# Hybrid attention encoder on one core: full-attention scores of two heads made together, the products with the low part of K over 64 rows each in two halves of the array

## Chip, cores, metric

The kernel runs on one core of one Trainium2 chip. The metric is device time in microseconds, the median of several runs. In the profile PE is TensorE (PEld its weight loads), DVE is VectorE, ACT ScalarE, POOL GpSimd, SP SyncE, whose queue issues most of the DMA transfers.

## What is computed

One layer of an encoder over 1024 tokens of width 1024. One input projection feeds two groups of heads: group A is full attention (8 query heads of 64 over 2 key heads, normalised and rotated), group B is attention over a neighbourhood on a grid. Both are gated, concatenated, projected and added to the residual. The part that matters here, cut from the reference:

```python
def _gqa_blocked(q, k, v):          # q: 8 heads, k and v: 2 heads, head_dim 64, 1024 tokens
    qb = q.reshape(b, nb, Q_BLOCK, hk, g, d)            # blocks of 128 queries
    def block(qi):
        sc = jnp.einsum('bqkgd,bskd->bkgqs', qi, k).astype(jnp.float32) * scale
        p = jax.nn.softmax(sc, axis=-1).astype(v.dtype)
        return jnp.einsum('bkgqs,bskd->bqkgd', p, v)
```

## The kernel before

Inputs are float32, and TensorE is fed with pairs of float16 numbers: a value is kept as a high part and a low part (what the high part leaves). A projection is three products: high x high, high x low, low x high.

Full attention is a list `ua` of 64 units in the order (hh, u, h): key head hh, block u of 128 queries, one of the four query heads h of that key head. The text calls unit i "head i" and the step in which it is started "step i". For one unit, `a_qk` makes the scores of 128 queries against 1024 keys in a PSUM tile `s` of two banks. The stationary operand `q` has 128 rows: the high part of the query's 64 numbers and the low part, stacked. The moving operand is first `kTa[:, :, hh]`, which holds the high part of K twice, one copy under the other (lines L713, two products of 512 columns: high and low part of q times the high part of K), then K's low part, also held twice (`kTa[:, :, 2]` for hh 0, `klo1` for hh 1; L715, two more products into the same banks). DVE reduces the scores to a row's maximum (L720, with a junk output), ACT makes the exponential in float32 (L722) and its float16 copy (L723), DVE subtracts to get the low part (L728, in `a_lo`, one step later), SP issues one transpose of both parts (L733), and five steps later `a_pv` multiplies with V (L745 to L747, 24 small products). The tiles `s` come from a pool with two buffers.

`Flow` sets the order. Each call of `fl.step` runs, for each engine in program order: pieces due "pre", ACT's jobs, `a_qk` followed by `a_pv` of the unit five back, `a_lo` of the unit before, pieces due "mid", DVE's jobs, and then a number of filler chunks (`fl.fill`). A chunk is six products of 256 columns or three of 512 of a projection that a later stage needs (L482); `FILL_A` and what follows it say how many go into a step (5, then 4.2, then about 3.7). Evacuations of these projections and the splitting of weights into high and low parts (ACT L392, DVE L397) are jobs. In the first six steps the order on ACT, DVE, POOL and SP is left to a list scheduler; from step 6 on it is the order of the program. PE's order is always that of the program.

The first steps overlap with the preparation of the last query tiles: `norm_rope` (DVE L533, L534, POOL L535, DVE L539, POOL L543, DVE L546, POOL L547) and then the staging in `qa_gen`: ACT L562 copies the high part, DVE L563 subtracts the low part, and L566 issues the transpose that puts both into `qTa`. The text calls the stretch from the first scores to 130 us "the head" of the stage.

Group B follows. Its `b_scores` makes scores of two heads together: two products of 128 rows (L804), and then two products of 64 rows with K's low part (L807), one on rows 0 to 63 and one on rows 64 to 127, for which an even head's staged query has its high part in the upper rows and an odd head's in the lower ones.

Of the kernel before, what the change touches and what calls it, by code (L numbers as in the profile page):

```python
# [8 lines left out]
F32 = mybir.dt.float32  # L9
F16 = mybir.dt.float16  # L10
BF16 = mybir.dt.bfloat16
AF = mybir.ActivationFunctionType
OP = mybir.AluOpType
# [3 lines left out]
P = 128  # L17
# [4 lines left out]
D = 64  # L22
# [17 lines left out]
RING, VB1 = 5, 24576  # L40
# [8 lines left out]
class Flow:  # L49
# [12 lines left out]
    def at(self, delay, pos, fn, *a):  # L62
        self.due.setdefault((self.slot + delay, pos), []).append((fn, a))
# [75 lines left out]
def kernel(ctx: ExitStack, tc: tile.TileContext, x: bass.AP, w: bass.AP, wo: bass.AP,  # L139
# [3 lines left out]
    act, dve, pool, pe, sp = nc.scalar, nc.vector, nc.gpsimd, nc.tensor, nc.sync  # L143
# [5 lines left out]
    ps_s = ctx.enter_context(tc.tile_pool(name="ps_s", bufs=2, space=PSUM))  # L149
# [4 lines left out]
    at, job = fl.at, fl.job  # L154
# [8 lines left out]
    ar = one.tile([P, 16928], F32, name="ar")  # L163
# [3 lines left out]
    def carve(store, off, shape, dt):  # L167

        n = 4 if dt == F32 else 2
        t = store[:, off // 4:off // 4 + int(np.prod(shape)) * n // 4]  # L170
        t = t if n == 4 else t.bitcast(dt)
        if len(shape) == 1:
            return t
        names = "abcdef"[:len(shape)]
        return t.rearrange(f"p ({' '.join(names)}) -> p {' '.join(names)}", **dict(zip(names, shape)))
# [6 lines left out]
    def slot(kind, shape, dt):  # L182

        off, size, n = SLOTS[kind]
        k = turn[kind] = turn.get(kind, -1) + 1
        off += k % n * size
        return area(off, shape[1:], dt) if off < AREA else carve(rq, off - AREA, shape[1:], dt)
# [4 lines left out]
    def r6(i, shape, dt, name):  # L192
        if i >= 2:
            return carve(rq, (i - 2) * 6144, shape[1:], dt)
        return one.tile(shape, dt, tag=f"r{i}", name=name)

    def tn(name, n=1, tag="t"):
        return tiny.tile([P, n], F32, tag=tag, name=name)
# [47 lines left out]
    NSA, SHA = 80, 81  # L246

    def col(i, n=1):
        return sm[:, i:i + n]
# [239 lines left out]
    def proj_pair(g, up, lhs, evac):  # L489

        need_w(g)
        pt = proj_tile(f"pj{g}_{up}")
        hi, lo = wp[g]
        trips = ((0, hi), (0, lo), (1, hi))
        if (g, up) in ((KVA, 0), (QA, 0)):
            seq = [(k, a, b) for a, b in ((0, hi), (1, hi), (0, lo)) for k in range(KC)]
        else:
            seq = [(k, a, b) for k in range(KC) for a, b in trips]
        for i in range(2):
            ops = [((pt[:, i], lhs(a, k, 2 * up + i), b[:, k]), dict(start=n == 0, stop=n == 23))  # L500
                   for n, (k, a, b) in enumerate(seq)]
            yield from chunks(ops, 6, (lambda: evac(pt)) if i else None)
# [4 lines left out]
    kTa = r6(0, [P, NU, 3, P], F16, "kTa")  # L507
# [5 lines left out]
    qTa = [carve(rq, 8192 * i, [NU, 4, P], F16) for i in range(2)]  # L513
    klo1 = carve(rq, 16384, [NU, P], F16)
# [39 lines left out]
    def qa_gen(hh, up):  # L554
        def evac(pt):
            g = QA + hh
            stg = slot("stg1", [P, 2, 4, P], F16)
            a, b = (0, D) if hh == 0 else (D, 0)

            def fin(q):  # L560
                d = 3 if hh else 2
                at(d, "pre", lambda: act.activation(stg[:, :, :, a:a + D], q, AF.Copy))  # L562
                at(d, "mid", lambda: dve.tensor_tensor(stg[:, :, :, b:b + D], q, stg[:, :, :, a:a + D], op=OP.subtract))  # L563

                def tr():
                    sp.dma_start_transpose(qTa[hh][:, 2 * up:2 * up + 2].rearrange("p i h t -> p (i h) t"),  # L566
                                           stg.rearrange("p i a b -> p (i a b)"))
                at(d, "post", tr)
            norm_rope(g, up, pt, 4, 0, fin)
        yield from proj_pair(QA + hh, up, from_h, evac)  # L570

    def kva_gen(up):
        def evac(pt):
            both = slot("stg1", [P, 8, P], F16)
            stg, stg_l = both[:, :6].rearrange("p (i a) b -> p i a b", a=3), both[:, 6:]
            vs = pt[:, :, P:].rearrange("p a (h d) -> p a h d", d=D)
            at(1, "pre", lambda: act.activation(va[:, 2 * up:2 * up + 2, :, :D], vs, AF.Copy, scale=2.0 ** -14))

            def vlo():
                for i in range(2):  # L580
                    dve.scalar_tensor_tensor(va[:, 2 * up + i, :, v_lo], vs[:, i], 2.0 ** -14,
                                             va[:, 2 * up + i, :, :D], op0=OP.mult, op1=OP.subtract)
            at(1, "mid", vlo)

            def fin(k):
                def hi():
                    act.activation(stg[:, :, :2, :D], k, AF.Copy)
                    act.activation(stg[:, :, :2, D:], k, AF.Copy)
                at(2, "pre", hi)

                def lo():
                    for h, to in ((0, stg[:, :, 2]), (1, stg_l)):
                        dve.tensor_tensor(to.rearrange("p i (e d) -> p i e d", d=D),
                                          k[:, :, h, None, :].to_broadcast([P, 2, 2, D]),
                                          stg[:, :, h].rearrange("p i (e d) -> p i e d", d=D), op=OP.subtract)
                at(2, "mid", lo)

                def tr():
                    sp.dma_start_transpose(kTa[:, 2 * up:2 * up + 2].rearrange("p i a t -> p (i a) t"),
                                           both[:, :6].rearrange("p a b -> p (a b)"))  # L600
                    sp.dma_start_transpose(klo1[:, 2 * up:2 * up + 2], stg_l.rearrange("p a b -> p (a b)"))
                at(2, "post", tr)
            norm_rope(KVA, up, pt[:, :, :P], 2, 1, fin)
        yield from proj_pair(KVA, up, from_h, evac)
# [94 lines left out]
    def group(g, gens):  # L699

        def first(gen):
            prep(g + 1)
            yield from gen
        return [first(gens[0]) if g < 16 else gens[0], *gens[1:]]


    pv, sums, pts, hls = {}, {}, {}, {}

    def a_qk(i, hh, u, h):
        s = ps_s.tile([P, 1024], F32, tag="s", name=f"s{hh}_{u}_{h}")  # L710
        q = qTa[hh][:, u, h]
        for c in range(2):
            pe.matmul(s[:, c * 512:(c + 1) * 512], q, kTa[:, 4 * c:4 * c + 4, hh], start=True, stop=False)  # L713
        for c in range(2):
            pe.matmul(s[:, c * 512:(c + 1) * 512], q, klo1[:, 4 * c:4 * c + 4] if hh else kTa[:, 4 * c:4 * c + 4, 2],  # L715
                      start=False, stop=True)
        nm = tn(f"nm{hh}_{u}_{h}")
        o = 4096 * (i % RING)
        hl, p32 = carve(ar, o, [2, 1024], F16), carve(ar, o + 2048, [1024], F32)
        dve.tensor_tensor_reduce(out=hl[:, 1].bitcast(BF16), in0=s, in1=col(SHA).to_broadcast([P, 1024]), scale=col(NSA),  # L720
                                 scalar=3e38, op0=OP.add, op1=OP.min, accum_out=nm)
        act.activation(p32, s, AF.Exp, bias=nm, scale=col(SCA))  # L722
        at(0, "mid", lambda: act.activation(hl[:, 0], p32, AF.Copy))  # L723
        hls[hh, u, h] = (hl, p32)

    def a_lo(i, hh, u, h):
        hl, p32 = hls.pop((hh, u, h))
        dve.tensor_tensor(hl[:, 1], p32, hl[:, 0], op=OP.subtract)  # L728
        if i % 4 == 3:
            pt = one.tile([P, 16, P], F16, tag="gain", name=f"pt{hh}_{u}_{h}")  # L730
        else:
            pt = carve(ar, 4096 * RING + 2048 + 4096 * (i % 4), [16, P], F16)
        sp.dma_start_transpose(pt, hl.rearrange("p a b -> p (a b)"))  # L733
        pts[hh, u, h] = pt
# [292 lines left out]
    k, q = [kva_gen(up) for up in UP], group(1, [qa_gen(0, up) for up in UP])  # L1027
# [86 lines left out]
    mid = (CHUNKS_A - sum(n * r for n, r in FILL_A) - FILL_A_END * SKEW_A) / (64 - n_head) + 0.02  # L1114
    fl.base = BASE_A
    with run_units(ua, SKEW_A, a_qk, a_lo, a_pv, rates(FILL_A + [(64 - n_head, mid)], FILL_A_END), by_hand=HAND):
        pass
# [39 lines left out]
    a, b = ORDER[2:4]  # L1157
# [112 lines left out]
```

## Time and profile before

| what | before |
|---|---|
| runs, us | 572.87, 575.61, 575.24; median 575.24 |
| span of the profiled execution, us | 570.8 (its own time isn't listed; the span leaves out what lies before the first and after the last instruction) |
| PE busy | 517.2 us, 91% of the span |
| DVE busy | 459.4 us, 80% |
| ACT busy | 391.7 us, 69% |
| full attention, first to last score product, us | 85.2 to 350.4 |

A busy PE means that some matmul is in flight. Matmuls overlap in the pipeline, so what one costs is read from the distance between starts, not from its duration. Rows of the timeline give start, duration, engine, line, operation, output<-input, shapes, how many instructions are merged, and in brackets how long the engine was idle before and what ended that.

### The profile page before, as it was taken

What the parts mean: (1) busy time and instruction counts of PE and PEld (TensorE: products, weight loads), DVE (VectorE), ACT (ScalarE), POOL (GpSimd) and SP (SyncE); (2) the same over time, 40 slices, a digit from 0 to 9 for tenths busy, and PEclk for the clock granted to TensorE, in tenths of its full rate; (3) what the DMA queues carried; (4) which work ended last, traced back from release to release, by engine and by line L of the source; (5) the groups of instructions that cost most, each with busy time, mean ns of one, the idle gap of its engine ahead of it and who ended that gap; (6) DMA issues with size and microseconds to landing.
All of it is one profiled execution on the core that took longest, in us unless ns stands there. A gap on an engine that the chain in (4) does not pass through costs nothing. (4 is left out here: it accounts for less than half of the span.)

```text
span 570.8 us, 13962 instructions
## 1 busy us (share of the span) xinstructions
PE 517.2 (91%) x5583; PEld 402.1 (70%) x5583; DVE 459.4 (80%) x1018; ACT 391.7 (69%) x615; POOL 150.6 (26%) x181
## 2 busy tenths in 40 slices
PE   2678889969999999999999999999799799997994
PEld 0456777757887555568888888887677577776883
DVE  4688787989887988778779887589978998988852
ACT  5546457667777769687696886387888888875321
POOL 2395786650000000000000022334521311212210
PEclk9979999998999999999999999999989899999998
DMA  8999548779999989998998999436466999899842
GB/s 241 220 175 231 121 91 185 131 144 165 220 180 210 158 204 200 197 196 162 217 191 192 184 160 213 132 52 130 121 121 107 198 216 165 144 176 167 194 109 73
DMA packets 245539, 95.49 MB, mean 167 GB/s; under 512 B 236513, under 2 KB 237025, under 8 KB 243554
## 3 DMA queue, kind: packets, MB, share of 16 engines
q1 hardware_dynamic: 241874, 73.89, 71.1%
q0 software_dynamic: 3312, 19.92, 12.7%
q10 hardware_dynamic: 288, 0.79, 0.5%
q8 instruction: 43, 0.70, 0.5%
q14 instruction: 22, 0.18, 0.1%
HBM read 29.56 MB, written 4.19 MB: 59 GB/s over the span
## 5 line engine op out<-in xcount | busy, mean ns | idle before, releaser
L482 PE MATMUL pj<-whl,hT 128*128 128x256 f16 x2112 | 254.9, 278 | 26.1 <-DMA hT<-ar 9.2
L482 PEld LDWEIGHTS <-hT 128*128 128x128 f16 x2112 | 203.7, 99 | 63.6 <-issue 20.3
L722 ACT ACTIVATE ar<-s,nm,sm 128x1024 f32<-128x1024 f32 x64 | 76.9, 1201 | 56.5 <-DVE nm L720 56.2
L720 DVE CUSTOM_DVE_ANT_0 ar<-s,sm 128x1024 bf16<-128x1024 f32 x64 | 82.0, 1281 | 35.0 <-PE s L715 34.6
L482 PEld LDWEIGHTS <-ar 128*128 128x128 f16 x768 | 73.0, 99 | 16.1 <-issue 7.0
L728 DVE TENSOR_TENSOR ar<-ar 128x1024 f16<-128x1024 f32 x64 | 80.3, 1255 | 0.9 <-ACT ar L723 0.8
L482 PE MATMUL po<-whl,ar 128*128 128x256 f16 x576 | 68.7, 273 | 2.0 <-DVE x2b L961 1.8
L723 ACT ACTIVATE ar<-ar 128x1024 f16<-128x1024 f32 x64 | 67.6, 1057 | 1.9
L828 ACT ACTIVATE rq<-ar,mx,sm 128x384 f32<-128x384 f32 (+1 forms) x64 | 43.0, 672 | 25.3 <-DVE mx L827 25.0
L829 ACT ACTIVATE ar<-ar,mx,sm 128x384 f16<-128x384 f32 (+1 forms) x64 | 43.5, 680 | 2.1
L482 PE MATMUL kb<-hT,whl 128*128 128x512 f16 x192 | 44.5, 379 | 0.0
L834 DVE TENSOR_TENSOR ar<-rq,ar 128x384 f16<-128x384 f32 (+1 forms) x64 | 35.5, 555 | 8.2 <-ACT ar L829 8.0
L746 PE MATMUL pv<-va,ar 128*128 128x64 f16 x384 | 40.6, 195 | 0.0
L745 PE MATMUL pv<-va,ar 128*128 128x65 f16 x384 | 40.5, 194 | 0.0
L747 PE MATMUL pv<-va,ar 128*128 128x65 f16 x384 | 40.4, 193 | 0.0
L713 PE MATMUL s<-kTa,rq 128*128 128x512 f16 x128 | 38.5, 383 | 1.5 <-ACT ar L722 1.4
L745 PEld LDWEIGHTS <-ar 128*128 128x128 f16 x384 | 35.9, 97 | 5.5 <-issue 0.3
L397 DVE SCALAR_TENSOR_TENSOR whl<-raw,sm,whl 128x512 f16<-128x512 f32 x52 | 39.5, 790 | 0.0
L746 PEld LDWEIGHTS <-ar 128*128 128x128 f16 x384 | 35.7, 98 | 5.5 <-issue 0.3
L207 POOL DMA_DIRECT2D raw<-in_w_dram x11 | 6.7, 607 | 113.0 <-ACT ar L723 88.8
L747 PEld LDWEIGHTS <-ar 128*128 128x128 f16 x384 | 35.7, 99 | 0.0
L392 ACT ACTIVATE whl<-raw,sm 128x512 f16<-128x512 f32 x52 | 33.9, 708 | 0.0
(163 smaller groups left out, 918.8 us busy)
## 6 DMA issues: line engine op xcount, KB each, us to landing
raw<-in_w_dram POOLq DMA_DIRECT2D x11, 1024.0 KB, 7.4
raw<-in_wo_dram POOLq DMA_DIRECT2D x4, 1024.0 KB, 5.7
ar<-in_x_dram SPq DMA_DIRECT2D x7, 512.0 KB, 6.3
khh<-ar SPq DMA_DIRECT2D x16, 128.0 KB, 3.5
x2b<-in_x_dram POOLq DMA_DIRECT2D x4, 512.0 KB, 6.1
x<-in_x_dram POOLq DMA_DIRECT2D x4, 512.0 KB, 5.8
out_dram<-x2b SPq DMA_DIRECT2D x8, 256.0 KB, 4.8
ar<-ar SPq DMA_TRANSPOSE x112, 4.3
```

What stands on the lines that cost most here:

```text
L397: dve.scalar_tensor_tensor(wp[g][1][:, q], raw[g][:, q], col(S_ + g), wp[g][0][:, q], op0=OP.mult, op1=OP.subtract)
L482: pe.matmul(*o[0], **o[1])
L713: pe.matmul(s[:, c * 512:(c + 1) * 512], q, kTa[:, 4 * c:4 * c + 4, hh], start=True, stop=False)
L720: dve.tensor_tensor_reduce(out=hl[:, 1].bitcast(BF16), in0=s, in1=col(SHA).to_broadcast([P, 1024]), scale=col(NSA), scalar=3e38, op0=OP.ad ...
L722: act.activation(p32, s, AF.Exp, bias=nm, scale=col(SCA))
L723: at(0, "mid", lambda: act.activation(hl[:, 0], p32, AF.Copy))
L728: dve.tensor_tensor(hl[:, 1], p32, hl[:, 0], op=OP.subtract)
L745: pe.matmul(o, pt[:, kt], va[:, kt, hh, v_hi], start=kt == 0, stop=False)
L746: pe.matmul(o[:, :D], pt[:, kt], va[:, kt, hh, v_lo], start=False, stop=False)
L747: pe.matmul(o, pt[:, 8 + kt], va[:, kt, hh, v_hi], start=False, stop=kt == 7)
L828: act.activation(p32, t, AF.Exp, bias=mx, scale=col(SCB + hh))
L829: act.activation(hl[:, 0], t, AF.Exp, bias=mx, scale=col(SCB + hh))
```

## The change

Scores are made for two units at once, at every even step, by a new function `a_scores`: four products with the high part of K (two per head), then the four with the low part, each over 64 rows: the even head's on rows 0 to 63, the odd head's on rows 64 to 127, alternating. Only the high part of q meets the low part of K now. DVE's reductions of both heads follow one another in that step; the exponential of the second head stays in its own step. For this the staged query of odd heads has its two parts swapped in `qa_gen`, which splits one ACT copy and one DVE subtraction into two each.

```diff
@@ qa_gen
-            a, b = (0, D) if hh == 0 else (D, 0)
+            s6 = stg.rearrange("p i (k e) (b d) -> p i k e b d", e=2, d=D)
...
-                at(d, "pre", lambda: act.activation(stg[:, :, :, a:a + D], q, AF.Copy))
-                at(d, "mid", lambda: dve.tensor_tensor(stg[:, :, :, b:b + D], q, stg[:, :, :, a:a + D], op=OP.subtract))
+                q5 = q.rearrange("p i (k e) d -> p i k e d", e=2)
+                for e in range(2):
+                    at(d, "pre", lambda e=e: act.activation(s6[:, :, :, e, e], q5[:, :, :, e], AF.Copy))
+                    at(d, "mid", lambda e=e: dve.tensor_tensor(s6[:, :, :, e, 1 - e], q5[:, :, :, e], s6[:, :, :, e, e], op=OP.subtract))
...
+    def a_scores(i, hh, u, hs):
+        k_lo = klo1 if hh else kTa[:, :, 2]
+        s = [ps_s.tile([P, 1024], F32, tag="s", name=f"s{hh}_{u}_{h}") for h in hs]
+        q = [qTa[hh][:, u, h] for h in hs]
+        for e in range(2):
+            for c in range(2):
+                pe.matmul(s[e][:, c * 512:(c + 1) * 512], q[e], kTa[:, 4 * c:4 * c + 4, hh], start=True, stop=False)
+        for c in range(2):
+            for e in range(2):
+                r = slice(e * D, e * D + D)
+                pe.matmul(s[e][:, c * 512:(c + 1) * 512], q[e][r], k_lo[r, 4 * c:4 * c + 4], start=False, stop=True)
+        for e, h in enumerate(hs):
+            nm = tn(f"nm{hh}_{u}_{h}")
+            o = 4096 * ((i + e) % RING)
+            hl, p32 = carve(ar, o, [2, 1024], F16), carve(ar, o + 2048, [1024], F32)
+            dve.tensor_tensor_reduce(out=hl[:, 1].bitcast(BF16), in0=s[e], in1=col(SHA).to_broadcast([P, 1024]), scale=col(NSA),
+                                     scalar=3e38, op0=OP.add, op1=OP.min, accum_out=nm)
+            hls[hh, u, h] = (hl, p32, s[e], nm)
+
     def a_qk(i, hh, u, h):
...
+        if h % 2 == 0:
+            a_scores(i, hh, u, (h, h + 1))
+        hl, p32, s, nm = hls[hh, u, h]
         act.activation(p32, s, AF.Exp, bias=nm, scale=col(SCA))
         at(0, "mid", lambda: act.activation(hl[:, 0], p32, AF.Copy))
-        hls[hh, u, h] = (hl, p32)
```

What moves, engine by engine. PE at head 26 (tile `s_6_2`; `s_6_3` is head 27, `pv_5` a probability product, `kb_1_0` a filler). Before, one head's four score products stand between a filler and a probability product:

```order
L482 MATMUL kb_1_0_2504<-hT_99,whl_1740 128x512
L713 LDWEIGHTS rq
L713 MATMUL s_6_2_2515<-kTa,rq 128x512
...
L713 MATMUL s_6_2_2515<-kTa,rq 128x512
L715 LDWEIGHTS rq
L715 MATMUL s_6_2_2515<-kTa,rq 128x512
...
L745 MATMUL pv_5_2457<-va,ar 128x65
```

After, at the same place, both heads' products (L717 with K's high part, L721 with the low part):

```order
L717 MATMUL s_6_2_2531<-kTa,rq 128x512
...
L717 MATMUL s_6_3_2532<-kTa,rq 128x512
...
L721 MATMUL s_6_2_2531<-kTa,rq 128x512
L721 LDWEIGHTS rq
L721 MATMUL s_6_3_2532<-kTa,rq 128x512
...
L756 MATMUL pv_5_2473<-va,ar 128x65
```

Head 27's four products moved up by one step, past the probability products and fillers of step 26, and step 27 has no scores.

DVE at the same place (ISA is the reduction, `nm` its result; L728, after the change L739, the subtraction of the head before). Before:

```order
L720 ISA ar,nm_6_2_2520<-s_6_2_2515,sm 128x1024
L720 ISA nm_6_2_2520 128x1
L728 TENSOR_TENSOR ar<-ar 128x1024
L651 SCALAR_TENSOR_TENSOR klo<-kb_0_1_2390,ar 128x512
L720 ISA ar,nm_6_3_2572<-s_6_3_2567,sm 128x1024
L720 ISA nm_6_3_2572 128x1
L728 TENSOR_TENSOR ar<-ar 128x1024
```

After:

```order
L726 ISA ar,nm_6_2_2541<-s_6_2_2531,sm 128x1024
L726 ISA nm_6_2_2541 128x1
L726 ISA ar,nm_6_3_2543<-s_6_3_2532,sm 128x1024
L726 ISA nm_6_3_2543 128x1
L739 TENSOR_TENSOR ar<-ar 128x1024
L653 SCALAR_TENSOR_TENSOR klo<-kb_0_1_2406,ar 128x512
L739 TENSOR_TENSOR ar<-ar 128x1024
```

The second reduction moved ahead of the subtraction and the evacuation of the even step.

DVE in the head of the stage, at heads 6 and 7 (`nt_3` belongs to the last query tile's norm). Before:

```order
L533 TENSOR_REDUCE nt_3_1132<-ar 128x8
L720 ISA ar,nm_1_2_1215<-s_1_2_1210,sm 128x1024
L720 ISA nm_1_2_1215 128x1
L534 TENSOR_SCALAR nt_3_1132<-nt_3_1132,sm 128x8
L728 TENSOR_TENSOR ar<-ar 128x1024
L563 TENSOR_TENSOR ar<-ar 128x8x64
L539 TENSOR_TENSOR ar<-ar,nt_3_1132 128x512
L546 TENSOR_TENSOR ar<-ar,tabs 128x512
L720 ISA ar,nm_1_3_1284<-s_1_3_1279,sm 128x1024
```

After:

```order
L533 TENSOR_REDUCE nt_3_1151<-ar 128x8
L534 TENSOR_SCALAR nt_3_1151<-nt_3_1151,sm 128x8
L726 ISA ar,nm_1_2_1233<-s_1_2_1223,sm 128x1024
L726 ISA nm_1_2_1233 128x1
L726 ISA ar,nm_1_3_1235<-s_1_3_1224,sm 128x1024
L726 ISA nm_1_3_1235 128x1
L739 TENSOR_TENSOR ar<-ar 128x1024
L565 TENSOR_TENSOR ar<-ar 128x4x64 x2
L539 TENSOR_TENSOR ar<-ar,nt_3_1151 128x512
```

Here the list scheduler and the pairing put the norm's second piece ahead of both reductions and the reduction of head 7 ahead of the rotation.

More of the change, by code (lines that the diff above doesn't have):

```diff
@@ L707 @@
     pv, sums, pts, hls = {}, {}, {}, {}
-    def a_qk(i, hh, u, h):
[L710 to L721, printed above, removed]
+    def a_scores(i, hh, u, hs):
[16 more added lines that the diff above has]
+            hls[hh, u, h] = (hl, p32, s[e], nm)
@@ L722, in a_qk @@
+    def a_qk(i, hh, u, h):
+        if h % 2 == 0:
+            a_scores(i, hh, u, (h, h + 1))
+        hl, p32, s, nm = hls[hh, u, h]
         act.activation(p32, s, AF.Exp, bias=nm, scale=col(SCA))
         at(0, "mid", lambda: act.activation(hl[:, 0], p32, AF.Copy))
-        hls[hh, u, h] = (hl, p32)
     def a_lo(i, hh, u, h):
-        hl, p32 = hls.pop((hh, u, h))
+        hl, p32 = hls.pop((hh, u, h))[:2]
         dve.tensor_tensor(hl[:, 1], p32, hl[:, 0], op=OP.subtract)
```

## The prediction

> **What bounds the kernel now.** I read the page first, then busy time by stretches of the span, then who waits for whom, then two steps of the full attention and one pair of scores of the neighbourhood attention in order of time.
>
> ```profile
> span 570.8 us, 13962 instructions
> PE 517.2 (91%) x5583; PEld 402.1 (70%) x5583; DVE 459.4 (80%) x1018; ACT 391.7 (69%) x615; POOL 150.6 (26%) x181
> PE   2678889969999999999999999999799799997994
> ```
>
> ```profile
> core 0: us, PE busy (x) PEld busy (x) DVE busy (x) ACT busy (x) POOL busy (x), PEclk, DMA share, GB/s
> 85.00:130.00 45.00, 39.27 (x387) 31.18 (x386) 38.47 (x56) 30.16 (x48) 28.27 (x22) 0.97 0.81 155
> 130.00:350.00 220.00, 220.00 (x2555) 161.62 (x2554) 184.04 (x320) 167.58 (x218) 12.21 (x25) 0.99 1.00 191
> ```
>
> ```profile
> ACT ar L722 <- DVE nm L720: 56.2, 41, 3.8
> DVE ar L720 <- PE s L715: 34.6, 42, 1.8
> PE pj L482 <- ACT ar L722: 4.2, 1, 4.2
> PE s L713 <- ACT ar L722: 1.4, 1, 1.4
> ```
>
> The full attention runs from the first score at 85.2 us to the last at 350.4. From 130 to 350 PE has no idle time, while DVE (184 of 220) and ACT (168) wait for it: DVE's reduction waits for scores 34.6 us in all, and the exponential waits for the reduction. There, less PE work is less time. The head (85 to 130) is different: PE idles 5.7 of 45 us, and the two waits of PE that stand in the list lie in it.
>
> **The change, part by part.** Two steps (heads 26 and 27) show the price of scores and the slack around them.
>
> ```profile
> 200.80 0.60 PE L713 MATMUL s<-kTa,rq 128*128 128x512 f16 x2
> 201.23 0.60 PE L715 MATMUL s<-kTa,rq 128*128 128x512 f16 x2
> 201.66 0.19 PE L745 MATMUL pv<-va,ar 128*128 128x65 f16 x1
> 201.97 1.27 DVE L720 CUSTOM_DVE_ANT_0 ar<-s,sm 128x1024 bf16<-128x1024 f32 x1
> 202.41 2.75 PE L482 MATMUL kb<-hT,whl 128*128 128x512 f16 x12
> 203.16 1.22 DVE L728 TENSOR_TENSOR ar<-ar 128x1024 f16<-128x1024 f32 x1
> 203.28 1.20 ACT L722 ACTIVATE ar<-s,nm,sm 128x1024 f32<-128x1024 f32 x1 [1.49 <-DVE nm L720]
> 204.51 1.06 ACT L723 ACTIVATE ar<-ar 128x1024 f16<-128x1024 f32 x1
> 205.00 0.60 PE L713 MATMUL s<-kTa,rq 128*128 128x512 f16 x2
> 205.43 0.60 PE L715 MATMUL s<-kTa,rq 128*128 128x512 f16 x2
> 206.59 2.10 PE L482 MATMUL kb<-hT,whl 128*128 128x512 f16 x9
> 208.64 0.59 PE L713 MATMUL s<-kTa,rq 128*128 128x512 f16 x2
> ```
>
> Starts, not durations, give the price: two products of 512 columns every 0.43 us, 0.215 each. A pair of heads costs 8 x 0.215 = 1.72 us of PE. After the change the four products with the high part of K stay (0.86), and the four with the low part become two rounds of two 64-row products. The neighbourhood attention has such a round already, with 384 columns:
>
> ```profile
> 443.30 0.49 PE L804 MATMUL sb<-khh,qTb 128*128 128x384 f16 x2 [0.26 <-DVE mx L825]
> 443.71 0.10 PEld L807 LDWEIGHTS <-qTb 64*128 64x128 f16 x2 [0.32 <-issue]
> 443.71 0.34 PE L807 MATMUL sb<-klo,qTb 64*128 64x384 f16 x2
> 443.98 0.39 PE L482 MATMUL pj<-whl,hT 128*128 128x256 f16 x2
> L807 PE MATMUL sb<-klo,qTb x64: 278/333/500, 370.2 to 517.0; 64*128 64x384 f16 x48, 64*128 64x256 f16 x16
> ```
>
> The two 64-row products take 0.34 us together where one takes 0.333 (median): they do run side by side. But going in and out costs. At 0.215 per 512 columns, 384 are worth 0.161; two full products should leave after 0.32 and the first 64-row weight load starts after 443.71 - 443.30 = 0.41, so 0.09 is lost going in; the round should last 0.161 and the next full product starts 0.27 later, so 0.11 is lost coming out. Together 0.20 us per pair, whatever the columns. With 384 columns that eats what a round saves (0.16); with two rounds of 512 it doesn't:
>
> - after: 0.86 + 0.09 + 2 x 0.215 + 0.11 = 1.49 us per pair, 0.23 less than 1.72.
> - Five of the 32 pairs (heads 0 to 9) lie in the head, where PE has idle time; there I count nothing. The other 27 lie where PE never idles: 27 x 0.23 = 6.2 us less.
>
> [...]
>
> What two rounds in a row cost between them no row shows. Lower bound nothing (full products follow each other every 0.215 with the weight load hidden); upper bound one more way out and in, 0.20 per pair, if the second load of a half waits until its first product has left. I take nothing, since a load of the same shape as its predecessor is hidden everywhere else in these rows; at the upper end 0.03 x 27 = 0.8 us remain.
>
> The new wait: the score tile has two buffers. Before, head i waited for the exponential of head i-2; now the second head of a pair waits for that of the head just before the pair. For heads 26 and 27, from the rows: the rounds end at 200.80 + 0.86 + 0.09 + 0.43 = 202.18; DVE started 0.31 after the last product left (201.97 against 201.66), so the reductions start at 202.49 and, 1.19 later, 203.68; the first exponential starts 1.31 after its reduction (203.28 against 201.97), 203.80, and takes 1.23 to the copy, 1.06; the second starts at 206.09 and ends at 207.3. PE leaves the scores at 202.29 and has the probability products and fillers of two steps, 205.00 - 201.66 = 3.34 and 208.64 - 205.86 = 2.78: it is back at 208.41, and the second head's first product is due at 208.84. Slack 1.5 us. Both copies and subtractions (L728) queue behind the longer reductions, but their transposes are wanted four steps later. DVE does the same work in 3% less time, 86% of it instead of 84%. I count no stall here.
>
> The transposes have to keep the new pace too:
>
> ```profile
> DMA to landing us min/median/max: 4.2/4.6/8.8
> L745 PE MATMUL pv<-va,ar 128*128 128x65 f16 x384 | 40.5, 194 | 0.0
> ```
>
> The probability products never wait for them, and the longest landing, 8.8 us, is two steps of the four. Nothing is counted; the cover that would have to go is some 8 us.
>
> The split of the query staging: eight ACT copies and eight DVE subtractions of 512 elements become two of 256 each.
>
> ```profile
> L563 DVE TENSOR_TENSOR ar<-ar 128x512 f16<-128x512 f32 x8 | 5.5, 687 | 2.1 <-ACT ar L562 2.1
> L754 DVE TENSOR_TENSOR ar<-pv,sum 128x256 f32<-128x256 f32 x16 | 6.8, 425 | 0.6
> L616 ACT ACTIVATE ar<-pj 128x256 f16<-128x256 f32 x16 | 5.1, 371 | 0.0
> L562 ACT ACTIVATE ar<-ar 128x512 f16<-128x512 f32 x8 | 5.0, 631 | 7.0 <-POOL ar L547 7.0
> ```
>
> ACT: 2 x 0.371 - 0.631 = 0.11 each, beside 7.0 us of idling for POOL, so nothing. DVE: 2 x 0.425 - 0.687 = 0.16 each; six of the eight lie in the head, where DVE is the busy engine: 1.0 us at most, 0 at least; I take 0.3, nearer the low end because DVE still idles 6.5 of the head's 45 us.
>
> The head itself:
>
> ```profile
> 119.85 0.59 PE L713 MATMUL s<-kTa,rq 128*128 128x512 f16 x2
> 126.16 0.63 ACT L562 ACTIVATE ar<-ar 128x512 f16<-128x512 f32 x1 [5.28 <-POOL ar L547]
> 127.22 1.21 ACT L722 ACTIVATE ar<-s,nm,sm 128x1024 f32<-128x1024 f32 x1
> 128.46 1.44 PE L482 MATMUL pj<-whl,hT 128*128 128x256 f16 x6 [4.23 <-ACT ar L722]
> 129.69 1.06 PE L713 MATMUL s<-kTa,rq 128*128 128x512 f16 x2
> 129.43 2.54 ACT L392 ACTIVATE whl<-raw,sm 128x512 f16<-128x512 f32 x4
> ```
>
> PE scores head 8 at 119.85, some 8.6 us before head 7's exponential ends (128.43), and only then stalls 4.2. Under the pair rule it can't score head 9 before 128.43, and step 8's products and fillers (4.0 us: 0.73 and five chunks of 0.65) would come behind it: at worst 4.2 us dearer. But the order of DVE changes as well: the last query tile's L533 and L534 now stand ahead of the reductions of heads 6 and 7, so POOL's chain (L535, L543, L547), for which ACT sat 5.28 us and head 7's exponential queued, starts one or two reductions (1.2 us each) sooner, which could gain up to 2 us. Between -2 and +4.2 I take 0.
>
> Sum: -6.2 + 0.3 + 0 = -5.9 us, span 570.8 to 564.9. The span is 2.1 to 4.8 us below the three times (572.87 to 575.61), and which of them is nearest to the profiled execution isn't shown; I take the difference as unchanged and put the sum to the median: 575.2 - 5.9 = 569.3. Bounds of the terms: -11.6 - 2 to -0.8 + 1.0 + 4.2.
>
> **Rivals.** (1) Rounds don't chain: 0.20 more per pair leaves 0.8 us; with the 0.3 the time is 574.7. For it: no row shows two rounds in a row; against: hidden loads elsewhere. (2) The second exponential becomes PE's limit, slower: 1.5 us of slack is gone where ACT splits a weight group in between, 2.54 us for four L392, which makes 1.0 us of wait; some seven groups fall into the stage: 7 us. With the head at +4.2 and some 2 us of slow clock after a longer idle (products of 0.59 took 1.06 at 129.69), 575.2 - 6.2 + 13.2 = 582. It decides once ACT has over 1.5 us of other work between a pair's exponentials; only four or five such places would leave no change. (3) Going in and out is free at this width: 27 x 0.43 = 11.6, 563.9; the rows at 443 speak against it. [...] (4) The transposes can't go faster (DMA share 1.00 from 130 to 350), PE then waits at L745 and nothing is gained, 575; against it: landings fall back to 4.2 us again and again.
>
> **How the numbers follow.** Forecast 0.60; rival 1, 0.11; rival 2, 0.13; rival 3, 0.06; rival 4, 0.10. About 0.5% (2.9 us) can be told from no change, so faster means below 572.3: the forecast (all but a head that costs its full 4.2) and rival 3, 0.64. Rivals 1 and 4 and the mild half of rival 2, with the forecast's rest, are the same: 0.27. The rest of rival 2 is slower: 0.09. The forecast's own range is 566 to 573; to leave out no more than 2 in 10 the range goes to 563.5, past rival 3's time, and to 576.
>
> **What would show it.** In the trace after: in a pair, the first weight load of 64 rows some 0.95 us after the pair's first score, the two rounds 0.215 apart, the first probability product about 0.54 after the first 64-row one; pitch of two steps 0.2 us shorter; PE still without idle time from 130 on, and DVE's wait for scores shorter. Wrong if PE waits at a pair's third score product for L722, if the second round starts 0.3 us or more after the first, if waits appear at L745's successor, or if the head ends later than 130 us.

## The result and the profile after

Slower by 0.9%. The kernel after takes 577.5 us (median), before 573.0 in the same comparison; the ratio is 1.0093, 95% interval 1.0065 to 1.0121. The forecast was 569.3 us, faster (5.9 us below the 575.2 of the three runs known then). The profiled execution of after has a span of 575.3 us, 4.5 more than before.

The page after and busy time by stretches, as for before:

```profile
span 575.3 us, 13971 instructions
PE 512.4 (89%) x5583; PEld 392.0 (68%) x5583; DVE 459.3 (80%) x1026; ACT 390.4 (68%) x623; POOL 152.2 (26%) x181
...
PE   2578989849999999999989999999798878998994
```

```profile
85.00:130.00 45.00, 36.11 (x357) 26.89 (x355) 37.29 (x60) 32.49 (x56) 29.20 (x22) 0.92 0.86 163
130.00:350.00 220.00, 215.44 (x2579) 152.65 (x2577) 184.10 (x322) 162.09 (x214) 12.19 (x25) 1.00 0.99 188
```

PE is busy 4.8 us less than before, which is what cheaper scores should do, and yet the span is longer: PE idles more. From 130 to 350 us it was never idle before; now 4.56 us are missing from 220. The list of waits (engine, tile, line, releaser; total us, times, longest) names who it waits for, and one wait that the kernel before doesn't list:

```profile
ACT ar L734 <- DVE nm L726: 26.3, 20, 2.8
ACT ar L735 <- DVE ar L739: 26.2, 29, 2.6
...
PE s L717 <- ACT ar L734: 13.4, 8, 7.4
```

L717 are the products with the high part of K, L721 the 64-row ones, L726 the reduction, L734 the exponential, L735 its float16 copy, L739 the subtraction. The copy now waits for a subtraction 29 times.

Four marks split the span: the first score, head 10's, head 62's, and the first score of the neighbourhood attention. The timeline rows of the last three marks, before and then after:

```profile
135.89 0.38 PE L713 MATMUL s<-kTa,rq 128*128 128x512 f16 x1
...
345.95 0.38 PE L713 MATMUL s<-kTa,rq 128*128 128x512 f16 x1
...
369.90 0.27 PE L804 MATMUL sb<-khh,qTb 128*128 128x256 f16 x1
```

```profile
136.74 0.38 PE L717 MATMUL s<-kTa,rq 128*128 128x512 f16 x1
...
346.94 0.38 PE L717 MATMUL s<-kTa,rq 128*128 128x512 f16 x1
...
370.67 0.38 PE L815 MATMUL sb<-khh,qTb 128*128 128x256 f16 x2
```

The same marks of all profiles, in us. "Head" is from the first score to head 10's, "middle" from head 10 to head 62, "B" from the first to the last 128-row score product of the neighbourhood attention. The last two columns are the median over all runs and the ratio to the kernel before on the same chip.

| kernel | first score at | head | middle | B | median | ratio, 95% |
|---|---|---|---|---|---|---|
| before | 85.23 | 50.66 | 210.06 | 146.9 | 573.0 | 1 |
| after | 85.33 | 51.41 | 210.20 | 151.6 | 577.5 | 1.0093 (1.0065, 1.0121) |
| e11 before, second profile | 85.49 | 50.08 | 210.07 | 147.8 | | |
| e8 after, second profile | 85.44 | 52.51 | 210.19 | 149.3 | | |
| e1 low products over 128 rows | 88.04 | 51.89 | 215.01 | 151.5 | 586.0 | 1.0211 (1.0181, 1.0241) |
| e2 subtraction first | 88.15 | 50.53 | 205.34 | 149.3 | 573.5 | 1.000 (0.9973, 1.0027) |
| e3 both exponentials first | 87.70 | 44.38 | 206.12 | 146.7 | 568.8 | 0.9913 (0.9882, 0.9944) |
| e4 heads 0 to 9 singly | 86.20 | 49.26 | 210.72 | 151.3 | 575.7 | 1.0035 (1.0009, 1.0061) |
| e5 ring places apart | 86.16 | 53.75 | 219.04 | 147.4 | 593.5 | 1.0336 (1.0291, 1.038) |
| e6 loads apart | 85.87 | 51.10 | 210.19 | 146.6 | 574.6 | 1.0038 (1.0016, 1.0061) |
| e7 e3 and e6 together | 86.58 | 45.80 | 205.89 | 147.0 | 565.4 | 0.9879 (0.9851, 0.9908) |
| e9 e7 with 128-row low products | 86.69 | 44.40 | 210.73 | 146.7 | 570.4 | 0.996 (0.994, 0.998) |
| e10 before, loads apart | 86.21 | 47.58 | 210.08 | 148.3 | 571.6 | 0.9986 (0.9965, 1.0006) |

Read the first two rows: the first score starts 0.1 us later, the head costs 0.75, the middle 0.14 where -6 was forecast, the last pair before B gains 0.22, B costs 4.7, and the end is 1.0 shorter. Together these are the 4.5 us. The middle has the same length to 0.02 us in every profile of one kernel; the head (47.6 to 50.7 with the same code in that stage) and B vary from run to run.

**A pair after the change.** Heads 38 to 41 in order of time, for PE (without probability products), DVE and ACT:

```profile
248.45 1.03 PE L717 MATMUL s<-kTa,rq 128*128 128x512 f16 x4
249.41 0.61 PE L721 MATMUL s<-rq 64*128 64x512 f16 x4
...
253.36 2.78 PE L482 MATMUL pj<-whl,hT 128*128 128x256 f16 x24
255.98 0.59 PE L717 MATMUL s<-kTa,rq 128*128 128x512 f16 x2
257.69 0.59 PE L717 MATMUL s<-kTa,rq 128*128 128x512 f16 x2 [1.11 <-ACT ar L734]
...
250.05 1.28 DVE L726 CUSTOM_DVE_ANT_0 ar<-s,sm 128x1024 bf16<-128x1024 f32 x1 [1.51 <-PE s L721]
...
251.26 1.28 DVE L726 CUSTOM_DVE_ANT_0 ar<-s,sm 128x1024 bf16<-128x1024 f32 x1
...
252.46 1.22 DVE L739 TENSOR_TENSOR ar<-ar 128x1024 f16<-128x1024 f32 x1
...
251.38 1.20 ACT L734 ACTIVATE ar<-s,nm,sm 128x1024 f32<-128x1024 f32 x1
253.78 1.06 ACT L735 ACTIVATE ar<-ar 128x1024 f16<-128x1024 f32 x1 [1.20 <-DVE ar L739]
254.74 0.58 ACT L652 ACTIVATE ar<-kb 128x512 f16<-128x512 f32 x1
255.22 1.32 ACT L392 ACTIVATE whl<-raw,sm 128x512 f16<-128x512 f32 x2
256.44 1.19 ACT L734 ACTIVATE ar<-s,nm,sm 128x1024 f32<-128x1024 f32 x1
```

Follow head 38. Its exponential ends at 252.58, and its copy doesn't start then: it waits 1.20 us for head 37's subtraction (252.46 to 253.68), which on DVE now stands behind the second reduction. The reason is in the code: `hl` and `p32` of a head are carved at `o` and `o + 2048` of a ring whose places are 4096 bytes apart, and `p32` is 4096 bytes long, so the float32 probabilities of head 37 lie over the place of head 38's float16 copy. Behind the copy come ACT's other jobs (0.58 and 1.32 us), and only then head 39's exponential, which ends at 257.63. PE wants head 39's score buffer again at 256.41 (0.43 after the pair's first product at 255.98) and gets it at 257.69.

### The profile page after: what moved, and what is told of

It is laid out like the page before. It is cut to its first block, busy times and chain, and to the rows that moved or that the text cites. A ratio compares the mean times of both kernels' runs of the same rounds, so it can differ in the third digit from the quotient of the medians.

```text
span 575.3 us, 13971 instructions
## 1 busy us (share of the span) xinstructions
PE 512.4 (89%) x5583; PEld 392.0 (68%) x5583; DVE 459.3 (80%) x1026; ACT 390.4 (68%) x623; POOL 152.2 (26%) x181
## 5 line engine op out<-in xcount | busy, mean ns | idle before, releaser
L726 DVE CUSTOM_DVE_ANT_0 ar<-s,sm 128x1024 bf16<-128x1024 f32 x64 | 79.7, 1281 | 30.1 <-PE s L721 30.1
L734 ACT ACTIVATE ar<-s,nm,sm 128x1024 f32<-128x1024 f32 x64 | 76.6, 1196 | 26.4 <-DVE nm L726 26.3
L735 ACT ACTIVATE ar<-ar 128x1024 f16<-128x1024 f32 x64 | 67.6, 1056 | 33.7 <-DVE ar L739 26.2
L739 DVE TENSOR_TENSOR ar<-ar 128x1024 f16<-128x1024 f32 x64 | 80.5, 1257 | 8.7 <-ACT ar L735 8.7
L717 PE MATMUL s<-kTa,rq 128*128 128x512 f16 x128 | 34.9, 382 | 13.4 <-ACT ar L734 13.4
L756 PEld LDWEIGHTS <-ar 128*128 128x128 f16 x384 | 35.3, 96 | 7.6 <-issue 6.4
L756 PE MATMUL pv<-va,ar 128*128 128x65 f16 x384 | 40.1, 194 | 0.0
L758 PE MATMUL pv<-va,ar 128*128 128x65 f16 x384 | 39.8, 192 | 0.0
L758 PEld LDWEIGHTS <-ar 128*128 128x128 f16 x384 | 35.4, 99 | 0.0
L876 POOL TENSOR_TENSOR ar<-ar 128x256 f32<-128x256 f32 x16 | 15.1, 943 | 71.9 <-DVE ar L874 56.9
```

What stands on the lines that cost most here:

```text
L726: dve.tensor_tensor_reduce(out=hl[:, 1].bitcast(BF16), in0=s[e], in1=col(SHA).to_broadcast([P, 1024]), scale=col(NSA), scalar=3e38, op0=OP ...
L756: pe.matmul(o, pt[:, kt], va[:, kt, hh, v_hi], start=kt == 0, stop=False)
L758: pe.matmul(o, pt[:, 8 + kt], va[:, kt, hh, v_hi], start=False, stop=kt == 7)
```

## Experiments

**e1: the 64-row part undone.** Only the low products change, the pairs stay.

```diff
-                pe.matmul(s[e][:, c * 512:(c + 1) * 512], q[e][r], k_lo[r, 4 * c:4 * c + 4], start=False, stop=True)
+                pe.matmul(s[e][:, c * 512:(c + 1) * 512], q[e], k_lo[:, 4 * c:4 * c + 4], start=False, stop=True)
```

> The changed kernel, but the low-part products of the pair run over all 128 rows (so the term low x low is in the sum again); order and pairing as changed. It undoes the 64-row half of the change alone. Theory (the 64-row rounds save what the rows said, 1.50 us a pair against 1.72, and the loss comes from the order): slower than the changed kernel's 577.5 by 0.22 us for each pair where PE is not waiting for an exponential, about 24 x 0.22 = 5 us, so 581 to 584; a pair's score products last 1.72 us and PE waits less for L734, since its later scores eat part of the wait. Rival (going in and out of 64 rows is what costs, in waits that the starts of products do not show): 577.5 or less.

Measured: 586.0 us, ratio 1.0211, above the 581 to 584 expected. The middle is 4.81 us longer than after's, 0.185 per pair and not 0.22: as expected, the dearer scores eat part of PE's waits, which are 0.9 us shorter in all. The first score also came 2.7 us later, as in the profiles of e2 and e3, before any edited product runs; why isn't settled, and that part of the 8.5 us says nothing of the rounds. So the 64-row rounds do save, and the loss has to come from the pairing around them.

**e2: the missed wait taken away on DVE.** The second head's reduction goes behind the subtraction of the head before.

```diff
-        for e, h in enumerate(hs):
+        def red(e, h):
...
+        red(0, hs[0])
+        at(0, "mid", red, 1, hs[1])
```

> The changed kernel with the second head's reduction put behind the subtraction of the head before, on DVE; all else the same. Theory: the float32 probabilities of head i lie over the next ring slot's high part, so the copy of head i (L735) has to wait until head i-1 is subtracted (L739), and the change had put a second reduction of 1.2 us ahead of that subtraction; with the order turned, L735 no longer waits for L739 (26.2 us in 29 waits in the changed kernel), the second exponential of a pair ends about 1.0 us earlier, PE's waits between 130 and 350 us fall from 4.6 to under 2, and the full attention ends 2 to 3 us earlier; the time is 573 to 576. Rival (ACT's own jobs between the two exponentials are the cause): L735's waits go, but PE waits 4 us or more as before, 577.

Measured: 573.5 us, ratio 1.000, as expected; the middle falls by 4.86 us to 205.34, and PE's idle time from 130 us to B from 4.56 to 0.36. ACT at the same place, heads 38 and 39 (scores from 249.68):

```profile
252.61 1.21 ACT L736 ACTIVATE ar<-s,nm,sm 128x1024 f32<-128x1024 f32 x1 [0.62 <-DVE nm L726]
253.84 1.06 ACT L737 ACTIVATE ar<-ar 128x1024 f16<-128x1024 f32 x1
254.81 0.58 ACT L652 ACTIVATE ar<-kb 128x512 f16<-128x512 f32 x1
255.28 1.32 ACT L392 ACTIVATE whl<-raw,sm 128x512 f16<-128x512 f32 x2
256.51 1.19 ACT L736 ACTIVATE ar<-s,nm,sm 128x1024 f32<-128x1024 f32 x1
```

The copy starts as soon as the exponential ends. With the same jobs behind it the second exponential starts 6.83 us after the pair's first score; after the change it was 7.99 (256.44 against 248.45). That 1.16 us is the missed wait. In the whole profile the copy still waits for the subtraction 15.1 us in 17 places, where the expectation had none; but all 17 are copies of a pair's second head, behind which no exponential of that pair stands, and PE hardly waits any more.

**e3: the second exponential ahead of the copy.**

```diff
-        hl, p32, s, nm = hls[hh, u, h]
-        act.activation(p32, s, AF.Exp, bias=nm, scale=col(SCA))
+            for g in (h, h + 1):
+                _, p, s, nm = hls[hh, u, g]
+                act.activation(p, s, AF.Exp, bias=nm, scale=col(SCA))
+        hl, p32 = hls[hh, u, h][:2]
```

> The changed kernel with both exponentials of a pair issued on ACT right after each other in the even step, ahead of the first head's copy and of the odd step's jobs; all else the same. Theory (the second exponential, queued behind the copy that waits and behind ACT's jobs, is what PE waits for): it ends about 5.4 us after the pair's first score instead of 7.5, PE's waits at L717 for the exponential fall from 13.4 us to under 4 in all, and the stall of 7.4 us at head 9 mostly goes; the full attention ends 8 us earlier than in the changed kernel, the time is 567 to 571. Rival 1 (the head of the stage is bound by DVE and POOL, whoever waits): only the 4.6 us behind 130 us come back, 572 to 574. Rival 2 (the 3.7 us that the changed kernel loses behind the full attention have a cause of their own and stay): 571 to 574 with the full attention ending 8 us earlier all the same.

Measured: 568.8 us, ratio 0.9913. The second exponential no longer stands behind a copy and ACT's jobs at all; the middle is 206.12 and the head 44.38, 7 us shorter than after's (e7 and e9, with the same order on ACT, have 45.80 and 44.40). It beats both kernels. Its profile is of its fastest run (564.8 us), 4 us under the median.

**e4: the pairs left out of the head.** Heads 0 to 9 are scored one at a time, over 128 rows (a branch for `i < 10` with the code of before).

> The changed kernel, but heads 0 to 9 are scored one at a time over 128 rows as before the change; pairs with 64-row rounds from head 10 on. Theory (in the first steps PE was up to 8.6 us ahead of the exponentials and the pair rule takes that lead away): PE is busy 39 of the 45 us from 85 to 130 again instead of 36, heads 10 and 11 start 2 to 3 us earlier than in the changed kernel, time 574 to 575.5. Rival (DVE and POOL bound the head anyway, as the prediction took): heads 10 and 11 start within 1 us of the changed kernel's 136.7, time 577.

Measured: 575.7 us, ratio 1.0035, just above what was expected. PE is busy 39.9 of the 45 us again. Head 10 starts at 135.5 instead of 136.7, 1.3 us earlier: less than the 2 to 3 expected, and more than the rival's 1. From the first score the head is 2.15 us shorter than after's (49.26), but the heads of one code differ by up to 3.1 us between profiles, so this one profile doesn't price the pairs there. The middle is 0.5 us longer, the rest as after.

**e5: the overlap itself taken away.** Successive heads lie three ring places apart.

```diff
-            o = 4096 * ((i + e) % RING)
+            o = 4096 * (3 * (i + e) % RING)
```

> The changed kernel with one number more: the probabilities of successive heads lie three ring slots apart instead of one, so the float32 probabilities of a head no longer lie over the place of the next head's float16 copy. Theory (the copy waits for the subtraction of the head before because of that overlap, and holds up the second exponential): ACT no longer waits for that subtraction at the copy (26.2 us in all in the changed kernel), PE's idle time from 130 us to the neighbourhood attention falls from 4.6 to under 1 us, the full attention from first score to the next stage's first score from 285.3 to 279.5 to 281.5 us, and the time, if the rest stays, from 577.5 to 572 to 574. Rival (the second exponential is late for another reason, ACT's other work): idle time and time as in the changed kernel, 576.5 to 578.5. Rival (the exponential now waits for the transpose of the head three back): ACT waits for DMA at the exponential, and the time is 577 or more.

Measured: 593.5 us, ratio 1.0336; the third of the expectations, more strongly than it said. The copy's wait for the subtraction is gone from the list, so the overlap was its cause. A new wait takes its place:

```profile
ACT ar L734 <- DMA ar<-ar: 24.9, 10, 5.8
...
PE s L717 <- ACT ar L734: 21.4, 8, 6.8
```

The exponential now writes over the place of the head three back, whose transpose hasn't landed; PE waits for the exponential as before, only longer. The ring's order had covered this.

**e8 and e11: both kernels again, unchanged.** Is B's loss chance?

> The changed kernel unchanged, a second profile. Theory (its long neighbourhood attention follows from the times at which loads and transposes meet, which the program sets): stage 150.5 to 152 us, a wait of PE for a transpose of 2 us or more between 455 and 470, time 576 to 578. Rival (it was chance in that one profile): stage 146.5 to 148.5 us and a time of 572 to 574.

> The kernel before unchanged, a second profile, to see what varies without any edit. Theory (the long neighbourhood attention belongs to the changed kernel's timing): that stage 146 to 148.5 us as in the first profile (146.9), PE's wait for a transpose near 464 us under 1 us; from the first score to head 10's 47 to 51 us; from head 10 to head 62 210.1 us again. Rival (the two kernels draw from the same lot there): 149 to 152 us with a wait of 2 us or more.

Measured: after 576.9 us, B 149.3; before 573.4 us, B 147.8. PE's waits for a transpose in B near 465 us, in the two profiles of after:

```profile
465.44 0.24 PE L862 MATMUL pvb<-rq,ar 128*128 128x65 f16 x1 [2.98 <-DMA ar<-ar]
```

```profile
467.47 0.24 PE L862 MATMUL pvb<-rq,ar 128*128 128x65 f16 x1 [2.33 <-DMA ar<-ar]
```

and in the two of before:

```profile
464.32 0.20 PE L851 MATMUL pvb<-rq,ar 128*128 128x65 f16 x1 [0.65 <-DMA ar<-ar]
```

```profile
464.18 0.20 PE L851 MATMUL pvb<-rq,ar 128*128 128x65 f16 x1 [0.93 <-DMA ar<-ar]
```

The two profiles of each kernel agree in kind (e8's B is shorter than the 150.5 expected, its wait is there). But the same B with the loads where they were also follows e1 to e4, and there it takes 146.7 to 151.5 us with waits at this place of 1.1 (e3) to 6.6 us (e4): the long B doesn't belong to every kernel with pairs. The wait of 2.98 us is followed by a clock of 0.50. Busy time and granted clock (the number after the five engines) of after:

```profile
460.00:465.00 5.00, 2.46 (x27) 1.55 (x24) 4.56 (x15) 4.87 (x12) 0.00 (x0) 0.95 1.14 216
465.00:471.00 6.00, 5.56 (x38) 3.76 (x38) 4.02 (x16) 4.42 (x8) 1.79 (x3) 0.50 1.22 175
```

From 465 to 471 us PE has 38 products; before has 70 in the same stretch, at 1.00.

**e6: the loads moved off the transposes.** The transposes in question are issued at 456 to 460 us, where POOL issues two loads of 512 KB back to back. One number moves one of them to 466.7 and the next to 470.9.

```diff
-            at(2, "end", next_load)
+            at(3, "end", next_load)
```

(in both places where it stands)

> The changed kernel with the residual's loads three steps apart instead of two, which moves one load of 512 KB from about 456.6 to about 466.5 us and the next from 466.5 to about 470. Theory (the neighbourhood attention lost 4.7 us because transposes issued at 456 to 460 land 8 us later beside two such loads, PE idles 3 us for them, and the clock is halved after that idle time): that wait falls below 1 us, the granted clock from 460 to 490 is 0.95 or more, the stage takes 147 to 148.5 us instead of 151.5, the time is 573 to 574.5 instead of 577.5. Rival (the loads are not what delays the transposes): stage 150.5 to 152, time 576.5 to 578.5. Rival (the later load delays others instead): a new DMA wait of PE after 470, time 576 or more.

Measured: 574.6 us, ratio 1.0038, 2.9 us less than after and just above what was expected. The two transposes issued between 457.5 and 460 us land after 5.6 and 6.3 us instead of 7.5 and 8.1, B is 146.6 us, the wait 1.14, a little more than expected, and the clock holds:

```profile
463.56 0.20 PE L862 MATMUL pvb<-rq,ar 128*128 128x65 f16 x1 [1.14 <-DMA ar<-ar]
...
465.00:471.00 6.00, 6.00 (x68) 4.56 (x67) 5.45 (x23) 4.61 (x8) 2.40 (x5) 1.00 0.75 146
```

**e10: the same in the kernel before.**

> The kernel before with the residual's loads three steps apart. Theory (before's neighbourhood attention meets the loads mildly: a 0.65 us wait in its profile): 0 to 2 us less than before, 570.5 to 572.5. Rival (before loses there as much as the changed kernel does in many of its runs): 568 to 570. It tells how much of the 7 us between before and the best version belongs to the loads alone.

Measured: 571.6 us, ratio 0.9986 with 1 inside the interval. Before loses little to those loads.

**e7 and e9: the best version, and the price of the 64-row rounds in it.** e7 is e3 and e6 together, e9 is e7 with e1's edit.

> Both exponentials ahead of the copies and the loads three steps apart: the two edits that single runs gave separately. Theory (both losses are separate): 564 to 567 us, 2 to 5 less than with the exponentials alone (568.8), and neighbourhood attention 146 to 148 us. Rival (the loads do not matter): 567.5 to 570.

> The kernel with both exponentials first and the loads three steps apart (565.4 us), but the products with the low part of K again over all 128 rows. It prices the 64-row rounds where the new waits are gone. Theory (a pair's scores cost 1.72 instead of 1.50 us and PE bounds the stage): 27 to 32 pairs of 0.22, 6 to 7 us more, 571 to 572.5. Rival (where PE waits anyway the dearer scores hide in waits): under 4 us more, 569 or less. Rival (they also eat the slack before the second exponential, as in the changed kernel, where full rows cost 8.5): 574 or more.

Measured: e7 565.4 us, ratio 0.9879; e9 570.4, ratio 0.996. e7 is the fastest of all, 12 us below the change as made by the medians; its interval overlaps e3's, so what moving the loads adds to e3 isn't clear of noise. e9 is 5.0 us slower than e7, between two of its expectations. Where no wait intervenes the price is the one worked out: from head 22 to head 62, e9 takes 161.24 us and e7 156.86, 4.38 for 20 pairs, 0.219 each. Over the whole middle the difference is 4.84 us, where 26 pairs of 0.219 make 5.69; the missing 0.85 us lies between heads 10 and 22, where e9 waits 0.5 us once that e7 doesn't, and e7 has one wait that e9 hasn't, in the step after head 20:

```profile
PE kb L482 <- DVE sum L764: 1.1, 1, 1.1
```

## Why the prediction was wrong

**Pair price (-6.2): right.** One pair without a wait, from the timeline (216.77 to 218.27):

```profile
216.77 1.03 PE L717 MATMUL s<-kTa,rq 128*128 128x512 f16 x4
217.73 0.61 PE L721 MATMUL s<-kTa,rq 64*128 64x512 f16 x4
218.27 0.20 PE L756 MATMUL pv<-va,ar 128*128 128x65 f16 x1
```

1.50 us against a forecast 1.49: the first 64-row products 0.96 after the first score (0.95 forecast), the rounds 0.23 apart (0.215), 0.31 from the second round to the probability product. Rival 1 (rounds don't chain) and rival 3 (free going in and out) are out. Rival 3's 0.43 us less per pair, from which the bound of -11.6 comes, no run shows: it would make the pair 1.29 us (6 x 0.215), and the pair took 1.50.

**The new wait ("I count no stall here"): the step that failed.** Ten pairs between head 14 and head 58 wait at the second head's first product, by 0.04 to 1.38 us, 5.79 in all beyond 1.50 each; the three profiles of that code in the middle give 5.79, 5.78 and 5.78. With 26 pairs of 0.219 saved this is 5.79 - 5.69 = +0.10, and the middle measured +0.14: this one term takes back the whole gain. e2, which removes the copy's wait ahead of the second exponential, gets back 4.86 of it. The slack of 1.5 us was worked out as if the copy followed the first exponential at once. The prediction saw that subtractions queue behind the longer reductions, but asked only when their transposes are wanted; it missed that ACT's next copy writes where the subtraction still reads. That takes 1.2 us of the slack, and then, by this estimate, an ordinary ACT job of 0.3 us or more is enough. Rival 2 named the right place, with 7 us for 5.8, but not the cause: it asked for 1.5 us of ACT's own work, and had a chance of 0.13.

**The head (taken as 0 between -2 and +4.2): +0.75, and +2.4 between the second profiles.** Both of its halves happened. The staging copy starts at 124.63 instead of 126.16, 1.5 us sooner, and the stall that the upper bound described came, larger:

```profile
125.78 1.21 ACT L734 ACTIVATE ar<-s,nm,sm 128x1024 f32<-128x1024 f32 x1
...
127.04 1.01 PE L717 MATMUL s<-kTa,rq 128*128 128x512 f16 x2 [7.44 <-ACT ar L734]
```

Head 9's product waits 7.44 us for head 7's exponential, and PE then runs slower for a while (these two products take 1.01 us, later pairs of them 0.59; the clock granted from 127.0 to 129.8 us is 0.50; from 85 to 130 us it is 0.92, before 0.97). That the term came out small is the balance of two large ones, so taking 0 was luck in part. What pairing costs there alone isn't settled (e4); e3, e7 and e9, where that exponential comes first, have heads 5.6 to 7.0 us shorter than after's.

**The split of the staging (+0.3).** DVE needs 6.0 us for it instead of 5.5, ACT 5.8 instead of 5.0; whether that lengthens the head by itself was not tried.

**Transposes in the full attention (0): right,** no probability product there waits: idle before L756 to L758 is 0.0 us (rival 4 out).

**What follows, taken as unchanged: wrong, B +4.7 in the first profiles and +1.4 between the second.** The prediction looked at landing times only inside the full attention. B has a place where transposes, two loads and a waiting PE meet with little slack; e6 gives back 2.9 us of the 4.5 between the medians. Why after meets it worse than before, when the issues of loads and transposes up to 456 us stand at the same distances in both, isn't settled, nor whether it does so by more than chance. In the first profile of after, PE was 1.2 us ahead of before at 456 us, and waited the longer for the next transpose; that fits the clock, 0.94 for before from 430 to 460 us and 1.00 for after, but isn't tested. The other 1.1 us of the longer wait are later issues and landings of the transposes.

## What to carry to other kernels

When two operations of one engine are moved together, ask of everything behind them who reads and who overwrites its data, by the byte addresses of buffers that are carved by hand, not by the names of the tiles: the wait that undid this change is in no dependence that the code spells out. Work out the slack of a double buffer with the longest jobs that can stand between, and order the engine that frees the buffer so that the freeing operation comes first (e3, -8.7 us against the change). And don't count a stage that isn't touched as unchanged before its length is compared in two profiles: B took 146.9 and 147.8 us before and 151.6 and 149.3 after, and 2.9 us of the time came back when two of its loads moved (e6).

## Of the hardware

A wait of PE for one transpose of 2.98 us was followed by a granted clock of 0.50 for 6 us, one of 2.33 us (e8) by 0.50 from 467.3 to 470.6 us, and waits of 0.65 (before), 0.93 (e11) and 1.14 us (e6) by 1.00 from 465 to 471 us. Half a clock for 6 us costs up to 3 us, by an estimate from these two figures, so the first of these waits was paid about twice. Near 412 us PE waits equally long (2.94 and 2.93 us) for the same DVE operation before and after, and the clock from 414 to 416 us is 0.50 before and 1.00 after; the six products behind the wait and the clock from 400 to 430 us, before and then after:

```profile
414.10 1.44 PE L482 MATMUL pj<-whl,hT 128*128 128x256 f16 x6 [2.94 <-DVE ar L687]
400.00:430.00 30.00, 26.66 (x285) 20.71 (x283) 26.48 (x75) 24.56 (x49) 12.23 (x15) 0.94 0.55 122
```

```profile
414.88 0.82 PE L482 MATMUL pj<-whl,hT 128*128 128x256 f16 x6 [2.93 <-DVE ar L689]
400.00:430.00 30.00, 26.41 (x293) 21.04 (x292) 26.55 (x71) 25.32 (x50) 12.49 (x13) 1.00 0.52 120
```

So a wait of 2.9 us was followed by half a clock in one of these profiles and not in the other, and a part of what B lost in the first profile of after may be chance.

In the pair at 216.77 us, entering the 64-row products cost 0.10 us (0.96 to the first of them, where four full ones take 0.86) and leaving 0.08 (0.31 from the last round to the probability product, where the rounds are 0.23 apart): once each for the two rounds, which follow each other in 0.23.
